# Gate/up and up products of four feed-forward layers by seven block products in place of eight

## The chip, the cores and the metric

The kernel runs on one core of a Trainium2 chip. The metric is device microseconds of one execution. Before the change, three executions took 2495.82, 2497.71 and 2503.09 us (median 2497.71).

## The reference

Two blocks of two layers work on one sequence of 512 tokens, model width 1024, float32. Each layer is a mixer (left as it is by the change) and a feed-forward part. In the first block that is (`hybrid_layer`, cut):

```
h = rms_norm(x, mlp_norm_w)
return x + jnp.square(jax.nn.relu(h @ w_up)) @ w_down      # w_up 1024x4096, w_down 4096x1024
```

and in the second (`swiglu`):

```
return (jax.nn.silu(h @ w_gate) * (h @ w_up)) @ w_down     # gate, up 1024x2816, down 2816x1024
```

where `h` is again an RMS norm of `x`, and the result is normalised once more and added to `x`.

## The kernel before

**Layout.** Activations lie feature-major: a tile has 128 features on the partitions and 512 tokens along the free dimension, so `x` is eight tiles `x[0..7]`. A weight tile `raw` is 128 by 1024: the eight 128x128 blocks (k = 0 to 7) that make one output tile of 128 features.

**Precision.** TensorE multiplies in fp32r. Every operand is split in two parts: `hi` (a copy rounded to fp32r, ScalarE) and `lo` (the rest, `raw - hi`, VectorE or GpSimd). `mm3` (lines 321 to 323) does hi·hi, hi·lo and lo·hi into one PSUM tile. So one output tile from eight k blocks is 24 matmuls of 512 columns, each with its own 128x128 weight load.

**Weights.** `weights` (lines 260 to 271) takes one of three `raw` buffers, loads it on SP's DMA queue, makes `whi` on ScalarE (line 268) and `wlo` on VectorE or GpSimd (line 269); `whi` and `wlo` have three buffers each.

**Feed-forward.** `mlp` (first block) makes 32 up tiles per layer: product, times the norm's reciprocal `rb` with a ReLU (VectorE, line 866), square (ScalarE, 867), split into an activation tile `act` (ScalarE, 275, and GpSimd, 276). `swiglu` (second block) makes 22 pairs of a gate and an up tile: each times `rb` (VectorE, 1235 and 1237), Silu (ScalarE, 1236), product of the two (VectorE, 1238), split. `groups` sets the order of the program: up tiles in groups (four of 8; 8, 8 and 6), two tiles of the next group made ahead, then eight down products over the group's activations, each added to `x` (line 874) or to `m` (1255, 1258). A scheduler then puts the instructions of each engine in a fixed order by its own estimates; each engine runs its list in that order, and waits on semaphores.

**Start of a feed-forward part.** `pre_norm` (first block) and `post_pre_norm` (second) split `x` times the norm's gain into `xg` (eight hi/lo pairs, lines 314 and 315) and work out `rb` from the sum of squares (GpSimd for the power, line 437; `rb` to SBUF on ScalarE, 461). The first three products run interleaved over k.

Of the kernel before, what the change touches and what calls it, by code (L numbers as in the profile page):

```python
# [79 lines left out]
def host_arrays(inp):  # L80
    g = {k: np.asarray(v) for k, v in inp.items()}
    out = {}

# [77 lines left out]
class Net:  # L161
# [696 lines left out]
    def mlp(self, l):  # L858
        nc, I, x = self.nc, self.I, self.x
        xg, _, rb = self.pre_norm("mlp_norm", l)  # L860

        def up(js):
            out = []
            for ps in self.fm_tiles([(self.weights(I["w1up"][l, j], 1024, nc.vector), 0) for j in js], xg):
                t, s = self.temp(), self.temp()
# [10 lines left out]
        self.groups([8] * 4, up, down)

    def groups(self, sizes, up, down, ahead=2, together=3):

        offs = np.cumsum([0] + list(sizes))  # L880
        done = {0: up(range(together)) + sum((up([j]) for j in range(together, sizes[0])), [])}
        for g in range(len(sizes)):
            if g + 1 < len(sizes):
                done[g + 1] = sum((up([offs[g + 1] + j]) for j in range(ahead)), [])
            down(g, done.pop(g))
            if g + 1 < len(sizes):
                done[g + 1] += sum((up([offs[g + 1] + j]) for j in range(ahead, sizes[g + 1])), [])

    def out_half(self, src, acts, into=None):

# [328 lines left out]
        self.normed_x = self.post_pre_norm(m, "mix_post", 1, "ffn_pre", 1)  # L1219

    def ffn(self, l):
        with self.phase(act=16, m=8):
            self.swiglu(l)

    def swiglu(self, l):
        nc, I = self.nc, self.I
        xg, rT, rb = self.normed_x

        def up(js):
            def ws(j):  # L1230
                return [(self.weights(I[n][l, j], 1024, nc.vector), 0) for n in ("gate", "up")]

            def product(pg, pu):
                t, u = self.temp(), self.temp()
                nc.vector.tensor_mul(t, pg, rb)  # L1235
                nc.scalar.activation(t, t, AF.Silu)
                nc.vector.tensor_mul(u, pu, rb)  # L1237
                nc.vector.tensor_mul(t, t, u)  # L1238
                return self.split(t, nc.gpsimd)

            if len(js) == 1:
                return [product(*(self.fm_tiles([w], xg)[0] for w in ws(js[0])))]
            (g0, u0), (g1, u1) = ws(js[0]), ws(js[1])
            p = self.fm_tiles([g0, u0, g1], xg)
            return [product(p[0], p[1]), product(p[2], self.fm_tiles([u1], xg)[0])]

        m = []

        def down(g, acts):
            for j in range(8):  # L1250
                src = I["down01"][l, g, j] if g < 2 else I["down2"][l, j]
                ps = self.fm_tile(self.weights(src, len(acts) * 128, nc.vector), acts)
                if g == 0:
                    t = self.get("m", S)
                    nc.scalar.activation(t, ps, AF.Copy)
                    m.append(t)
                else:
                    nc.vector.tensor_add(m[j], m[j], ps)

        self.groups([8, 8, 6], up, down, together=2)  # L1260
# [29 lines left out]
```

## Time and profile before

| | |
|---|---|
| median of three executions | 2497.71 us |
| the profiled execution | 2494.83 us, of which the span of its instructions is 2493.0 us |
| TensorE matmul busy | 2404.7 us, 96% |
| VectorE, ScalarE, GpSimd busy | 1360.7, 1039.4, 619.0 us (55%, 42%, 25%) |
| mean granted TensorE clock | 0.992 |
| moved by DMA | 215.30 MB, 86 GB/s |

Busy time of TensorE counts pipelined matmuls, whose rows overlap: the pace is the distance between the starts of two matmuls, not the length of a row.

### The profile page before, as it was taken

Reading aid. Unit: us, or ns where it says so; the run is one execution under the profiler, and the core shown is the slowest. Engines: PE = TensorE matmul, PEld = TensorE weight load, DVE = VectorE, ACT = ScalarE, POOL = GpSimd, SP = SyncE. Lnnn points to the kernel's source line nnn. Section 1 sums busy time; section 2 is a strip of 40 time slices with the busy share of each in tenths; the row PEclk is TensorE's granted clock in tenths of the full one; section 3 lists DMA queues with packets and bytes.
Section 4 is the critical chain, followed back from the end, with each engine's and each line's share of the span. In section 5 each row is a group of like instructions: output and inputs, shape, how many; then the busy total and the mean of one; then the engine's idle time right before and its main releaser. Section 6 shows DMA issues by size and latency. Waiting matters only on the chain.

```text
span 2493.0 us, 29049 instructions
## 1 busy us (share of the span) xinstructions
PE 2404.7 (96%) x11217; PEld 1950.8 (78%) x11217; DVE 1360.7 (55%) x2217; ACT 1039.4 (42%) x1625; POOL 619.0 (25%) x435
## 2 busy tenths in 40 slices
PE   9899999999998999999999999999999989999997
PEld 7787788888877878888887886888886766888886
DVE  6978643333488786333347867333336765433334
ACT  5656642232365675332233564223223563322222
POOL 3465320011045742110112531100001542100101
PEclk9999999999999999999999999999999999999998
DMA  4311132222232112222222211222222322322221
GB/s 160 106 64 47 64 102 93 95 100 93 77 104 91 60 47 86 100 93 93 93 97 77 84 52 60 97 98 94 93 83 70 95 75 68 102 96 98 94 87 66
DMA packets 61513, 215.30 MB, mean 86 GB/s; under 512 B 6848, under 2 KB 6976, under 8 KB 61376
## 3 DMA queue, kind: packets, MB, share of 16 engines
q1 hardware_dynamic: 59760, 207.06, 25.0%
q0 software_dynamic: 1472, 6.29, 0.7%
q8 instruction: 88, 1.44, 0.2%
q14 instruction: 49, 0.40, 0.1%
q10 hardware_dynamic: 144, 0.11, 0.0%
HBM read 211.33 MB, written 2.10 MB: 86 GB/s over the span
## 4 chain that ended last, share of the span: by engine, by line
PE 78%; DVE 14%; ACT 4%; issue 3%; POOL 1%; DMA 0%; ACTq 0%; DVEq 0%; POOLq 0%
PE mm L323 24%; PE mm L322 24%; PE mm L321 24%; DVE x L946 1%; DVE score L647 1%; PE st L307 1%; DVE m L646 1%; PE st L308 1%; PE st L542 1%; DVE m L1143 1%; ACT xg L314 1%; DVE act L287 1%; PE av L416 1%; DVE hs L1172 1%; PE av L491 1%
## 5 line engine op out<-in xcount | busy, mean ns | idle before, releaser
L268 ACT ACTIVATE whi<-raw 128x1024 fp32r<-128x1024 f32 (+3 forms) x398 | 409.8, 1032 | 1116.7 <-PE mm L322 934.6
L323 PE MATMUL mm<-xg,wlo 128*128 128x512 f32 x1792 | 711.5, 398 | 1.7 <-DVE wlo L269 1.7
L321 PE MATMUL mm<-xg,whi 128*128 128x512 f32 x1792 | 699.1, 394 | 14.3 <-ACT xg L314 12.1
L322 PE MATMUL mm<-xg,whi 128*128 128x512 f32 x1792 | 711.3, 397 | 0.2
L321 PE MATMUL mm<-act,whi 128*128 128x512 f32 x1160 | 455.8, 395 | 11.4 <-ACT act L275 8.5
L322 PE MATMUL mm<-act,whi 128*128 128x512 f32 x1160 | 459.8, 397 | 1.4 <-POOL act L276 1.4
L323 PE MATMUL mm<-act,wlo 128*128 128x512 f32 x1160 | 460.3, 397 | 0.0
L276 POOL TENSOR_TENSOR act<-t,act 128x512 fp32r<-128x512 f32 x108 | 150.4, 1395 | 1105.6 <-ACT act L275 1077.3
L269 DVE TENSOR_TENSOR wlo<-raw,whi 128x1024 fp32r<-128x1024 f32 (+2 forms) x289 | 348.4, 1207 | 135.8 <-ACT whi L268 135.3
L321 PEld LDWEIGHTS mm<-xg,whi 128*128 128x128 f32 x1792 | 339.5, 190 | 99.1 <-ACT xg L314 20.3
L322 PEld LDWEIGHTS mm<-xg,whi 128*128 128x128 f32 x1792 | 337.1, 188 | 82.9 <-DVE xg L315 6.6
L323 PEld LDWEIGHTS mm<-xg,wlo 128*128 128x128 f32 x1792 | 336.7, 188 | 76.2 <-DVE wlo L269 4.1
L269 POOL TENSOR_TENSOR wlo<-raw,whi 128x1024 fp32r<-128x1024 f32 (+3 forms) x109 | 257.3, 2362 | 296.0 <-ACT whi L268 284.7
L321 PEld LDWEIGHTS mm<-act,whi 128*128 128x128 f32 x1160 | 220.4, 190 | 64.6 <-ACT act L275 10.9
L322 PEld LDWEIGHTS mm<-act,whi 128*128 128x128 f32 x1160 | 218.3, 188 | 54.3 <-DVE act L276 2.3
L323 PEld LDWEIGHTS mm<-act,wlo 128*128 128x128 f32 x1160 | 218.1, 188 | 47.4
L874 DVE TENSOR_TENSOR x<-x,mm 128x512 f32<-128x512 f32 x64 | 44.0, 688 | 206.2 <-PE mm L323 206.2
L866 DVE SCALAR_TENSOR_TENSOR t<-mm,rb 128x512 f32<-128x512 f32 x64 | 44.1, 691 | 198.8 <-PE mm L323 198.6
L1237 DVE TENSOR_TENSOR t<-mm,rb 128x512 f32<-128x512 f32 x44 | 30.4, 691 | 141.8 <-PE mm L323 141.8
L1235 DVE TENSOR_TENSOR t<-mm,rb 128x512 f32<-128x512 f32 x44 | 30.4, 691 | 118.1 <-PE mm L323 118.1
L275 ACT ACTIVATE act<-t 128x512 fp32r<-128x512 f32 x114 | 72.1, 633 | 50.2 <-DVE t L1238 32.9
L307 PE MATMUL st<-act,act 128*128 128x128 f32 (+3 forms) x208 | 72.2, 356 | 20.8 <-DVE act L287 8.8
(226 smaller groups left out, 2641.5 us busy)
## 6 DMA issues: line engine op xcount, KB each, us to landing
raw<-in_w1up SPq DMA_DIRECT2D x64, 512.0 KB, 3.3
raw<-in_w1down SPq DMA_DIRECT2D x64, 512.0 KB, 3.2
raw<-in_gate SPq DMA_DIRECT2D x44, 512.0 KB, 3.3
raw<-in_up SPq DMA_DIRECT2D x44, 512.0 KB, 3.2
raw<-in_w1fm SPq DMA_DIRECT2D x41, 512.0 KB, 3.3
raw<-in_down SPq DMA_DIRECT2D x32, 512.0 KB, 3.2
raw<-in_odin SPq DMA_DIRECT2D x16, 512.0 KB, 3.3
raw<-in_w1out SPq DMA_DIRECT2D x16, 384.0 KB, 3.0
```

Of the source, the lines that this page charges most:

```text
L268: nc.scalar.activation(hi[:, sl], raw[:, sl], AF.Copy)
L269: (low or nc.gpsimd).tensor_sub(lo[:, sl], raw[:, sl], hi[:, sl].bitcast(F))
L275: nc.scalar.activation(hi, t, AF.Copy)
L276: (low or nc.vector).tensor_sub(lo, t, hi.bitcast(F))
L307: mm(ps, a[:, rows], b[hh][:, cols], start=True, stop=False, skip_group_check=True)
L321: mm(ps, w[0], a[0], start=first, stop=False, skip_group_check=True)
L322: mm(ps, w[0], a[1], start=False, stop=False, skip_group_check=True)
L323: self.last_mm = mm(ps, w[1], a[0], start=False, stop=last, skip_group_check=True)
L866: nc.vector.scalar_tensor_tensor(t, ps, 0.0, rb, op0=OP.max, op1=OP.mult)
L874: nc.vector.tensor_add(x[j], x[j], ps)
L1235: nc.vector.tensor_mul(t, pg, rb)
L1237: nc.vector.tensor_mul(u, pu, rb)
```

## The change

A pair of output tiles (up tiles j and j+1 in `mlp`, gate and up tile j in `swiglu`) times the 512 tokens is seen as a 2x2 block product: weights a11, a12 (first tile, k = 0 to 3 and 4 to 7), a21, a22 (second tile); tokens b11, b12 (k = 0 to 3, tokens 0 to 255 and 256 to 511), b21, b22 (k = 4 to 7). Eight block products become seven, with sums ahead and behind (`seven`; in the new listing its products are numbered here 1 to 7 in the order of the code). A block product is 12 matmuls of 256 columns.

- `token_sums`, once per layer: ScalarE copies `x` times the gain (8 of 128x512), GpSimd makes 16 sums of 128x256, then 4 splits of 128x1024 (ScalarE `tok` hi, VectorE `tok` lo).
- `pair_weights`, once per pair: the two `raw` tiles; GpSimd makes four sums of 128x512 (s1, s2 in one buffer, s3, s4 in another; two such buffers, `sum`); splits of a11|a12 (`whi`, `wlo`), s1|s2 and s3|s4 (`shi`, `slo`, three buffers in `mlp`, two in `swiglu`) and a22.
- `seven`: three PSUM tiles, seven products; a copy to `r` and one to `t` on ScalarE, five adds of 128x256 on VectorE; `post` then works from SBUF.
- Pairs run interleaved: products 1 to 3 of a pair, then 6 and 7 of the pair before, then 4 and 5.
- Per layer 13 pairs of up tiles in `mlp` (tiles 0 to 3, 30 and 31 stay plain) and 19 pairs in `swiglu` (j = 0, 1 and 21 stay plain): 64 pairs in all. They come in runs of 3, 4, 4 and 2 (`mlp`) and 5, 6, 6 and 2 (`swiglu`), between them a group's down products.
- The down products of the second block come in groups of 6, 6, 6 and 4 activations (before 8, 8 and 6), with weights of 128x768 and 128x512.
- The descriptor scratch is 4096 bytes in place of 8192; `act` has 10 and 8 buffers in place of 20 and 16.

The diff, cut:

```diff
+    def token_sums(self, x, g):
+        nc, out = self.nc, []
+        for k in range(4):
+            b = [self.temp() for _ in range(2)]
+            for i in range(2):
+                nc.scalar.activation(b[i], x[k + 4 * i], AF.Copy, scale=g(k + 4 * i))
+            (b11, b12), (b21, b22) = [(t[:, :256], t[:, 256:]) for t in b]
+            f = self.get("sum", 2 * S)
+            t1, t2, t3, t4 = [f[:, 256 * i:256 * i + 256] for i in range(4)]
+            nc.gpsimd.tensor_sub(t1, b12, b11)
+            nc.gpsimd.tensor_sub(t2, b22, t1)
+            nc.gpsimd.tensor_sub(t3, b22, b12)
+            nc.gpsimd.tensor_sub(t4, b21, t2)
+            t = self.get("tok", 4 * S, R)
+            hi, lo = t[:, :2 * S], t[:, 2 * S:]
+            nc.scalar.activation(hi, f, AF.Copy)
+            nc.vector.tensor_sub(lo, f, hi.bitcast(F))
+            out.append((hi, lo))
+        return out
...
+        a1 = parts(r0[:, :1024], 1024, ("whi", "wlo"))
+        p, q = self.get("sum", 2 * S), self.get("sum", 2 * S)
+        s1, s2, s3, s4 = p[:, :S], p[:, S:], q[:, :S], q[:, S:]
+        nc.gpsimd.tensor_add(s1, a21, a22)
+        nc.gpsimd.tensor_sub(s2, s1, a11)
+        s12 = parts(p, 1024, ("shi", "slo"))
+        nc.gpsimd.tensor_sub(s3, a11, a21)
+        nc.gpsimd.tensor_sub(s4, a12, s2)
+        s34 = parts(q, 1024, ("shi", "slo"))
+        a2 = parts(a22, 512, ("whi", "wlo"))
...
+        product(p1, a1, 0, plain(0, 0), True)
+        product(p2, s12, 1, summed(1), True)
+        product(p3, s12, 0, summed(0), True)
+        nc.scalar.activation(r1, p1, AF.Copy)
+        nc.vector.tensor_add(r2, p2, r1)
+        yield
+        t, u = self.temp(), self.temp()
+        product(p1, a1, 1, plain(1, 0), False)
+        product(p2, s34, 0, summed(2), False)
+        nc.scalar.activation(t[:, half[0]], p1, AF.Copy)
+        nc.vector.tensor_add(r3, p2, r1)
+        nc.vector.tensor_add(u[:, half[1]], p3, r3)
+        yield
+        product(p2, a2, 0, summed(3), False)
+        product(p3, s34, 1, plain(1, 1), False)
+        nc.vector.tensor_add(u[:, half[0]], p2, r1)
+        nc.vector.tensor_add(t[:, half[1]], p3, r2)
+        post(t, u)
+        yield
...
+        def both(j):
+            def post(t, u):
+                nc.vector.tensor_mul(t, t, rb)
+                nc.vector.tensor_mul(u, u, rb)
+                product(j, t, u)
+            return self.seven([I[n][l, j] for n in ("gate", "up")], xg, tok, post)
+
+        def pairs(js):
+            for j in js:
+                now = both(j)
+                next(now)
+                finish()
+                next(now)
+                left.append(now)
...
+        p = self.fm_tiles([plain("gate", 0), plain("up", 0), plain("gate", 1)], xg)
+        tok = self.token_sums(self.x, lambda c: self.v("ffn_pre", 8 * l + c))
+        product(0, tile(p[0]), tile(p[1]))
+        product(1, tile(p[2]), tile(self.fm_tiles([plain("up", 1)], xg)[0]))
+        pairs(range(2, 6))
+        for g, n in enumerate((6, 6, 6, 4)):
+            if g < 3:
+                pairs([6 * g + 6])
+            down(g, n, 0)
+            finish()
+            for j in range(1, 8):
+                down(g, n, j)
+            if g < 2:
+                pairs(range(6 * g + 7, 6 * g + 12))
```

What the scheduler's order makes of it shows at three places. Line numbers in the new order are those of the changed file: 386 and 387 are the hi and lo of a split in `pair_weights`, 393 to 397 its sums, 426 to 439 the copies and adds of `seven`, 359 to 370 `token_sums`, 1366, 1367 and 1353 the multiplications of `post`, 553 is `rb`.

VectorE, first layer of the second block, one pair in a run of gate/up tiles. Before:

```order
L1235 TENSOR_TENSOR t_13246<-mm_13196,rb_12731 128x512
L269 TENSOR_TENSOR wlo_13264<-raw_13261,whi_13263 128x1024
L1237 TENSOR_TENSOR t_13247<-mm_13221,rb_12731 128x512
L1238 TENSOR_TENSOR t_13246<-t_13246,t_13247 128x512
L269 TENSOR_TENSOR wlo_13329<-raw_13326,whi_13328 128x1024
```

Now (the pair whose s3|s4 is `slo_15756` is n, the one whose sums are `slo_15880` is n+1, and `t_15708`, `t_15709` are results of n-1):

```order
L387 TENSOR_TENSOR slo_15756<-sum_15746,shi_15755 128x1024
L438 TENSOR_TENSOR t_15709<-mm_15634,r_15636 128x256
L387 TENSOR_TENSOR wlo_15872<-raw_15867,whi_15871 128x1024
L439 TENSOR_TENSOR t_15708<-st_15635,r_15636 128x256
L1367 TENSOR_TENSOR t_15709<-t_15709,rb_14297 128x512
L1366 TENSOR_TENSOR t_15708<-t_15708,rb_14297 128x512
L387 TENSOR_TENSOR slo_15880<-sum_15875,shi_15879 128x1024
L1353 TENSOR_TENSOR t_15708<-t_15708,t_15709 128x512
L433 TENSOR_TENSOR r_15766<-mm_15764,r_15766 128x256
L387 TENSOR_TENSOR wlo_15890<-raw_15869,whi_15889 128x512
L434 TENSOR_TENSOR t_15839<-st_15765,r_15766 128x256
L427 TENSOR_TENSOR r_15896<-mm_15894,r_15896 128x256
```

Five instructions have become twelve, and the lo part of the next pair's s1|s2 stands behind the lo of this pair's s3|s4 and the results of the last.

GpSimd, the same run. Before, five pairs:

```order
L276 TENSOR_TENSOR act_13181<-t_13175,act_13181 128x512
L276 TENSOR_TENSOR act_13252<-t_13246,act_13252 128x512
L276 TENSOR_TENSOR act_13323<-t_13317,act_13323 128x512
L276 TENSOR_TENSOR act_13394<-t_13388,act_13394 128x512
L276 TENSOR_TENSOR act_13465<-t_13459,act_13465 128x512
```

Now, one pair and the first two sums of the next:

```order
L393 TENSOR_TENSOR sum_15745<-raw_15739 128x512
L394 TENSOR_TENSOR sum_15745<-sum_15745,raw_15737 128x512
L276 TENSOR_TENSOR act_15575<-t_15448,act_15575 128x512
L396 TENSOR_TENSOR sum_15746<-raw_15737,raw_15739 128x512
L397 TENSOR_TENSOR sum_15746<-raw_15737,sum_15745 128x512
L393 TENSOR_TENSOR sum_15875<-raw_15869 128x512
L394 TENSOR_TENSOR sum_15875<-sum_15875,raw_15867 128x512
```

One instruction per pair has become five; `sum_15746` takes the buffer from which the `slo` of the pair before was made.

ScalarE, start of the first `mlp`. Before:

```order
L461 ACTIVATE rb_3173<-av_3267 128x512
L867 ACTIVATE t_3290<-t_3289 128x512
L275 ACTIVATE act_3293<-t_3290 128x512
L867 ACTIVATE t_3297<-t_3296 128x512
L275 ACTIVATE act_3300<-t_3297 128x512
L867 ACTIVATE t_3304<-t_3303 128x512
L275 ACTIVATE act_3307<-t_3304 128x512
L268 ACTIVATE whi_3426<-raw_3424 128x1024
```

Now, from the second token split on (`rb_3173` stands twelve rows ahead of the first row):

```order
L369 ACTIVATE tok_3328<-sum_3323 128x1024
L359 ACTIVATE t_3331<-x_83,vec_sb 128x512
L359 ACTIVATE t_3332<-x_87,vec_sb 128x512
L359 ACTIVATE t_3343<-x_84,vec_sb 128x512
L359 ACTIVATE t_3344<-x_88,vec_sb 128x512
L369 ACTIVATE tok_3340<-sum_3335 128x1024
L369 ACTIVATE tok_3352<-sum_3347 128x1024
L958 ACTIVATE t_3386<-t_3386 128x512
L426 ACTIVATE r_3421<-mm_3418 128x256
L275 ACTIVATE act_3389<-t_3386 128x512
L386 ACTIVATE whi_3493<-raw_3489 128x1024
L386 ACTIVATE shi_3404<-sum_3400 128x1024
```

The copies of `x`, the four token splits and the first pair's `shi` come behind `rb`; in the second block the weights of the fourth plain product (`whi_14478`) come behind all four token splits in the same way.

## Rows read from the trace of the kernel before

**Rows 1.** The page, busy time by engine: us, share of the span, instructions.
```profile
PE 2404.7 (96%) x11217; PEld 1950.8 (78%) x11217; DVE 1360.7 (55%) x2217; ACT 1039.4 (42%) x1625; POOL 619.0 (25%) x435
```
**Rows 2.** The page, the chain that ended last, by engine.
```profile
PE 78%; DVE 14%; ACT 4%; issue 3%; POOL 1%; DMA 0%; ACTq 0%; DVEq 0%; POOLq 0%
```
**Rows 3.** TensorE in two stretches: 96 matmuls of 256 columns; 355 of 512 (feed-forward).
```profile
core 0: us, PE busy (x), PEclk, DMA share, GB/s
1376.70:1388.05 11.35, 11.34 (x96) 1.00 0.34 109
1558.00:1640.00 82.00, 82.00 (x355) 1.00 0.29 97
```
**Rows 4.** ScalarE groups by shape: count, then busy us, mean ns; last a timeline row.
```profile
L268 ACT ACTIVATE whi<-raw 128x1024 fp32r<-128x1024 f32 x351 | 371.1, 1059 | 1031.5 <-PE mm L322 874.4 <-issue 138.8 <-PE mm L323 6.5
L275 ACT ACTIVATE act<-t 128x512 fp32r<-128x512 f32 x114 | 72.1, 633 | 50.2 <-DVE t L1238 32.9 <-DVE t L1008 10.6 <-DVE pr L1000 3.2
L314 ACT ACTIVATE xg<-x,vec_sb 128x512 fp32r<-128x512 f32 x56 | 39.7, 717 | 56.4 <-DVE x L946 51.9 <-DVE x L856 4.5
...
1552.68 1.28 ACT L1236 ACT_TABLE_LOAD   x1 [1.91 <-DVE t L1235]
```
**Rows 5.** VectorE groups by shape; the third reads one operand from PSUM.
```profile
L269 DVE TENSOR_TENSOR wlo<-raw,whi 128x1024 fp32r<-128x1024 f32 x264 | 324.4, 1230 | 123.1 <-ACT whi L268 122.6
L1238 DVE TENSOR_TENSOR t<-t,t 128x512 f32<-128x512 f32 x44 | 30.4, 692 | 5.6 <-ACT t L1236 1.7
L547 DVE TENSOR_TENSOR pl<-st,ph 128x256 fp32r<-128x256 f32 x32 | 13.2, 413 | 1.8 <-ACT ph L546 1.8
```
**Rows 6.** GpSimd groups by shape.
```profile
L269 POOL TENSOR_TENSOR wlo<-raw,whi 128x1024 fp32r<-128x1024 f32 x87 | 215.9, 2482 | 248.3 <-ACT whi L268 237.0 <-issue 8.3 <-DVE mn L524 2.9
L276 POOL TENSOR_TENSOR act<-t,act 128x512 fp32r<-128x512 f32 x108 | 150.4, 1395 | 1105.6 <-ACT act L275 1077.3 <-issue 28.3
L276 POOL TENSOR_TENSOR pl<-t,ph 128x256 fp32r<-128x256 f32 x8 | 7.0, 876 | 11.9 <-ACT ph L275 11.7
```
**Rows 7.** Timelines, VectorE beside GpSimd at three moments: start us, us, engine.
```profile
331.23 3.81 POOL L276 TENSOR_TENSOR act<-t,act 128x512 fp32r<-128x512 f32 x3 [9.23 <-ACT act L275]
334.51 1.61 DVE L269 TENSOR_TENSOR wlo<-raw,whi 128x1024 fp32r<-128x1024 f32 x1 [0.36 <-ACT whi L268]
...
1529.59 1.29 POOL L406 TENSOR_TENSOR acc<-acc,t 128x512 f32<-128x512 f32 x1 [1.97 <-ACT t L400]
1529.62 1.80 DVE L946 TENSOR_TENSOR x<-x,m 128x512 f32<-128x512 f32 x1
...
1590.07 1.22 DVE L269 TENSOR_TENSOR wlo<-raw,whi 128x1024 fp32r<-128x1024 f32 x1
1590.90 1.54 POOL L276 TENSOR_TENSOR act<-t,act 128x512 fp32r<-128x512 f32 x1 [9.61 <-ACT act L275]
```
**Rows 8.** DMA issues: KB each, median us from issue to landing.
```profile
raw<-in_gate SPq DMA_DIRECT2D x44, 512.0 KB, 3.3
```
**Rows 9.** Timelines at the start of the first `mlp` and the first `swiglu`.
```profile
327.99 0.60 ACT L461 ACTIVATE rb<-av 128x512 f32<-128x512 f32 x1
329.14 2.08 DVE L866 SCALAR_TENSOR_TENSOR t<-mm,rb 128x512 f32<-128x512 f32 x3
333.46 0.69 DVE L866 SCALAR_TENSOR_TENSOR t<-mm,rb 128x512 f32<-128x512 f32 x1 [2.25 <-PE mm L323]
...
1546.87 1.02 POOL L437 TENSOR_TENSOR rstd<-var,mhalf 128x4 f32<-128x4 f32 x1 [6.22 <-DVE var L422]
1549.79 0.50 PE L323 MATMUL mm<-xg,wlo 128*128 128x512 f32 x1 [0.25 <-DVE wlo L269]
```
**Rows 10.** Windows: all five engines' busy time, then the clock; below, TensorE alone.
```profile
1530.00:1536.00 6.00, 4.40 (x17) 2.81 (x17) 5.74 (x6) 2.49 (x4) 2.16 (x2) 1.00 0.00 0
...
2034.00:2043.00 9.00, 0.72 (x2) 0.76 0.19 58
2043.00:2050.00 7.00, 7.00 (x26) 0.82 0.00 0
```

More of the change, by code (lines that the diff above doesn't have):

```diff
@@ L574, in hybrid @@
             self.mixers(l)
-        with self.phase(act=20):
+        with self.phase(act=10, tok=4, sum=2, shi=3, slo=3, r=2):
             self.mlp(l)
@@ L876, in mlp @@
[L876 to L887, printed above, removed]
+        acts = {}
@@ new lines, in down, with finish @@
+        def down(g, j):
+            ps = self.fm_tile(self.weights(I["w1down"][l, g, j], 1024, nc.vector), [acts[8 * g + k] for k in range(8)])
+            nc.vector.tensor_add(x[j], x[j], ps)
+        left = []
+        def pairs(js):
[5 more added lines that the diff above has]
+                left.append(now)
+        def finish():
+            while left:
+                next(left.pop())
+        up(range(3))
@@ L1221, in ffn @@
     def ffn(self, l):
-        with self.phase(act=16, m=8):
+        with self.phase(act=8, m=8, tok=4, sum=2, shi=2, slo=2, r=2):
             self.swiglu(l)
@@ L1227, in swiglu @@
         xg, rT, rb = self.normed_x
[L1229 to L1260, printed above, removed]
+        acts, m, left = {}, [], []
@@ new lines, in product, with tile, plain, both @@
+        def product(j, t, u):
+            nc.scalar.activation(t, t, AF.Silu)
+            nc.vector.tensor_mul(t, t, u)
+            acts[j] = self.split(t, nc.gpsimd)
+        def tile(ps):
+            t = self.temp()
+            nc.vector.tensor_mul(t, ps, rb)
+            return t
+        def plain(n, j):
+            return self.weights(I[n][l, j], 1024, nc.vector), 0
+        def both(j):
+            def post(t, u):
[3 more added lines that the diff above has]
+            return self.seven([I[n][l, j] for n in ("gate", "up")], xg, tok, post)
@@ new lines, in pairs, with finish, down @@
+        def pairs(js):
+            for j in js:
+                now = both(j)
+                next(now)
+                finish()
+                next(now)
+                left.append(now)
+        def finish():
+            while left:
+                next(left.pop())
+        def down(g, n, j):
+            src = I["down012"][l, g, j] if g < 3 else I["down3"][l, j]
+            ps = self.fm_tile(self.weights(src, n * 128, nc.vector), [acts[6 * g + k] for k in range(n)])
+            if g == 0:
+                t = self.get("m", S)
+                nc.scalar.activation(t, ps, AF.Copy)
+                m.append(t)
+            else:
+                nc.vector.tensor_add(m[j], m[j], ps)
@@ new lines, in swiglu @@
+        p = self.fm_tiles([plain("gate", 0), plain("up", 0), plain("gate", 1)], xg)
[4 more added lines that the diff above has]
+        for g, n in enumerate((6, 6, 6, 4)):
+            if g < 3:
+                pairs([6 * g + 6])
+            down(g, n, 0)
+            finish()
+            for j in range(1, 8):
+                down(g, n, j)
+            if g < 2:
+                pairs(range(6 * g + 7, 6 * g + 12))
+            elif g == 2:
+                pairs([19, 20])
+                t = tile(self.fm_tile(plain("gate", 21)[0], xg))
+                finish()
+                product(21, t, tile(self.fm_tile(plain("up", 21)[0], xg)))
```

71 lines of the change are left out of this document (57 added, 14 removed).

## The prediction, made before the changed kernel ran

> **What bounds the kernel now.** The page first: TensorE is busy 96% of the span, the others 25 to 55% [rows 1], and the chain that ended last runs over TensorE for 78% [rows 2]. The feed-forward stretches are solid matmul: 355 of 512 columns in 82.00 us, one each 0.231 us; 96 matmuls of 256 columns elsewhere in the kernel take 11.35 us, one each 0.119 us [rows 3]. So columns can be saved at half the price of a 512. Averages of the other engines say little: the question is which wait ends last inside a pair, for which I read the groups by shape [rows 4 to 6], the places where VectorE and GpSimd meet [rows 7], and the starts of the feed-forward parts [rows 9].
>
> **The change, part by part.**
>
> *Matmuls.* A pair cost 48 x 0.231 = 11.09 us and now has 84 x 0.119 = 10.00 us of matmul (one block product 1.43). That is 1.09 us each, 64 pairs, **-70 us** if nothing waits. The Trainium skill, "TensorE: Matmul & The Clock Gate", section "Back-to-back issue gap", gives about 131 ns for a sustained matmul of 512 columns with its weight load and 81 ns for 128. An estimate between them, 98 ns at 256, would make a pair go from 48 x 131 = 6.3 us to 84 x 98 = 8.2 us, and the change a loss of 123 us by itself. The trace differs at both widths measured here, and the measurement decides.
>
> *Work beside it, per gate/up pair.* VectorE: three lo splits of 1.23, one of 0.69, five adds of 0.41, three multiplications of 0.69 [rows 5]: 8.5 us. GpSimd: four sums and one activation, 1.29 each when undisturbed [rows 7]: 6.5 us. ScalarE some 5.7. Each is below 10 us alone; three things spoil it.
>
> *The port.* A VectorE instruction with both inputs in SBUF and a GpSimd instruction do not overlap: an add beside a GpSimd sum took 1.80 us, 0.54 after GpSimd's end; a `wlo` of 1.23 took 1.61 and ended 1.08 after GpSimd's (335.04); the other way round, a GpSimd split of 1.29 ended 1.15 after the `wlo` it met [rows 7]. VectorE reading PSUM shows no such stretching (0.41 for 256 columns, [rows 5]).
>
> *Buffers and queues.* In `swiglu` `shi` has two buffers, so s3|s4 of pair n can be split only after product 7 of pair n-1, two products before it is needed; s1|s2 of n+1 stands behind it on ScalarE and VectorE. `sum` has two buffers, so GpSimd's s3 of n+1 starts when the `slo` of n is done. I follow one cycle from T, the issue of the last matmul of product 7 of n-1 (us): result seen 0.22; hi of s3|s4 +1.06 = 1.28; lo +1.22 and a hop = 2.55. There GpSimd takes the port for s3, to 3.9. VectorE's next add reads PSUM; its `wlo` for a1 of n+1 then ends at 3.9 + 1.08 = 4.95. s4 takes the port in the shadow of the second PSUM add, to 6.1; the two multiplications of the pair before end at 6.65 and 7.3, the `slo` of s1|s2 at **8.55**. TensorE has meanwhile done product 4, waited 0.9 for the lo of product 5, some 1.1 for `wlo` in product 1, and stands at the third matmul of product 2; 46 matmuls are left to the next product 7: 46 x 0.119 = 5.47. A cycle is 14.0, taken as 14.1, against 10.0: 4.1 lost. Behind s4 GpSimd waits for the next raw tile: its buffer is free at 6.1, landing takes 3.3 [rows 8], two sums end by 12, before they are needed; the load is hidden, with 2 us to spare. The cycle repeats in a run of b pairs b-2 times: 3+4+4+0 = 11 per layer, 22 in all: **+90 us**. The last pair of each of the 8 runs still waits 1.0 for its lo: **+8**.
>
> In `mlp` `shi` has three buffers. In a run's first cycle only `wlo` of a1 is late (hi 1.28, hi of a1 2.34, `slo` 2.55, add 2.96, `wlo` 4.2 where product 1 wants it at 3.1): +1.2. In the second, the last pair's second raw tile lands at 4.2 + 3.3 = 7.5, then two activation splits and two sums go over GpSimd (4 x 1.29, to 12.7), hi of the sums 13.8, hi of a1 14.9, and `wlo` after s4 has left the port, 17.2 against 14.1: +3.3 with the hops. Runs of 3, 4, 4, 2: 10 per layer, **+20**.
>
> *Token sums.* 16 sums of 128x256 on GpSimd; none like it but [rows 6]'s third, 0.88; half of 1.29 is 0.65. I take 0.75, so 12 us per layer, and they begin late. First `mlp`, as ScalarE's order has them behind `rb` (328.6, [rows 9]): ReLU from 329.1, square, copy [rows 4]: the first sum at 331.2. Then three activation splits stand on GpSimd, to 336.4; 15 sums (11.2), 2.3 for lo splits that take the port, 2.2 for copies of `x` that stand behind a token split on ScalarE: 352.1. s1 and s2 of the first pair 2.6 and 1.1 of port: 355.8; hi 357; lo behind another `wlo` 359.3. TensorE has done its plain tiles at 333.2 (VectorE takes the last at 333.46 [rows 9]) and has 32 matmuls more that it may do, 3.8 us: it stands 22 us. The second pair's sums, behind these, cost 5 more. In `swiglu` the fourth plain product began before 1549.8 [rows 9], from 1548.8; now its weights stand on ScalarE behind all token splits: reciprocal root at 1547.9, 16 sums 12, waits for copies and port 4.5, hi 1.06, table load 1.28, Silu 0.63, hi of the weight 1.06 = 1568.5: 20 us. Two of each: **+94**. After a standstill of nine us the granted clock averaged 0.82 over the next seven [rows 10], 2.5 us at 1.2 in place of 2.4 GHz, 1.3 us lost; four times: **+5**.
>
> *At nothing.* Down products: the same 528 matmuls per layer; 8 more loads, splits and adds (0.69) lie under products of 18 x 0.231 = 4.2 us and, in the last group, 2.8 us; uncovered, the adds would cost 8 x 0.69 x 2 = 11 us. The smaller scratch serves GpSimd's few DMAs in the mixers.
>
> **Sum.** -70 + 90 + 8 + 20 + 94 + 5 = +147 on the profiled execution's 2494.8, so 2642; the median stands 2.9 above it. I forecast **2645 us**.
>
> **Rivals.**
> (1) *All of it is covered, faster.* The place is the stretch from product 7 to the `slo` of s1|s2. If it took 4.5 us (10.0 - 5.47) or less in place of 8.55, and the token sums fitted under the plain products, -70 remains: 2428. It decides at 5.6 us, where a pair costs its old 11.09. For it: no engine has 10 us of work per pair. Against it: the order puts five VectorE and two GpSimd instructions into that stretch, and their durations are rows.
> (2) *The port costs nothing*, because GpSimd's sums happen to fall under PSUM adds and idle time. The cycle is then the plain sum, 12.65 (+2.65, 58), `mlp` 16, starts 22 and 16 (76): -70 + 58 + 8 + 16 + 76 + 5 = +93: 2591. For it: in the trace of before most `wlo` rows run at 1.23 [rows 5]; against it, GpSimd had one split per pair then and has five or six now.
> (3) *The starts cost half*, if the token sums go under plain products better than the queues say: 2598.
> (4) *The clock falls inside the runs.* TensorE stands some 4 of 14 us. At 1.2 GHz the 46 matmuls of a cycle take 5.5 us more, 22 cycles, 120 us: 2765. Against it: at 4.40 busy of 6.00 the clock stayed at full speed [rows 10].
>
> **How the numbers follow.** Forecast 0.56, (2) 0.18, (3) 0.10, (4) 0.05; (1) 0.08; a cover that by chance just pays for the saving, no change, 0.03. Some 0.3% is what a measurement of this kernel can tell from none. So faster 0.08, the same 0.03, slower 0.89. The range takes in (2) and (3) and half of each start and cycle cost below, 2555; above, token sums at 0.88 (+2 per start and the port waits that come with them, 15), one more GpSimd instruction per cycle in VectorE's way (22 x 1.25 = 27) and `mlp` runs twice as late (20): 2707, set at 2710.
>
> **What would show it.** Right: products of 256 columns at 0.119; gaps on TensorE before the third matmul of product 2 of some 2.4 us, ended by line 387 of VectorE; runs of gate/up pairs with product 7 every 14 us; `slo`, `wlo` and multiplications stretched beside lines 393 to 397 of GpSimd; 20 us and more of TensorE idle at the start of each feed-forward part, ended by the pair's `shi` or the fourth product's `whi`. Wrong: a spacing above 0.132 per matmul (11.09 / 84), which would be TensorE's own loss; product 7 every 10 us; a full TensorE at the starts.

## The result, and the profile after

The changed kernel takes 2598.45 us (median of 4 runs, 2592.7 to 2604.44) against 2500.4 for the kernel before in the same comparison: a ratio of **1.0394, 95% interval 1.0363 to 1.0425**. It is slower, as forecast, by 98 us where the forecast was 147. The profiled execution has a span of 2590.8 us, 97.8 more than the one before.

Busy time by engine and the chain that ended last, from the page of the changed kernel; they answer to [rows 1] and [rows 2].

```profile
PE 2375.4 (92%) x13521; PEld 2040.4 (79%) x13521; DVE 1702.5 (66%) x2713; ACT 1216.1 (47%) x1945; POOL 1062.8 (41%) x755
...
PE 63%; DVE 21%; ACT 5%; POOL 5%; issue 5%; DMA 1%; POOLq 0%; ACTq 0%; DVEq 0%; SPq 0%
```

TensorE's share of the chain fell from 78% to 63%, VectorE's rose from 14% to 21% and GpSimd's from 1% to 5%: TensorE now waits for the work beside it. For what it waits, the view of TensorE's waits says (us in total, times, the longest); the first, second and fifth of these rows have no counterpart before, the third one of 1.1 us.

```profile
PE mm L323 <- DVE slo L387: 38.9, 26, 2.4
PE mm L321 <- ACT r L426: 34.2, 3, 17.0
PE mm L321 <- ACT whi L268: 32.6, 3, 16.0
PE mm L321 <- ACT xg L314: 12.1, 15, 0.8
...
PE mm L323 <- DVE wlo L387: 7.8, 4, 2.0
```

The first row is nearly all the runs of gate/up pairs, the second the starts of the two `mlp` layers, the third those of the two `swiglu` layers, the fifth the runs of up/up pairs; the fourth stood there before.

For a ledger I added up the starts of successive matmuls over each whole trace. A step that is over 0.35 us longer than usual for its width counts as a wait, the smaller excess as stretched. Sorted by the granted clock, 10 us of the stretched are matmuls at the lower clock before, 36 after; the rest is small excess at full clock, much the same in both.

| us | usual spacing | waits | stretched |
|---|---|---|---|
| before | 2340 | 86 | 63 |
| after | 2270 | 224 | 94 |

So the saving is there in full, -70, and 138 us of waits and some 30 of stretched matmuls, 26 of them at the lower clock, are laid on it: +98.

**A cycle of gate/up pairs.** Four engines around one cycle in the first `swiglu`, from its timelines (start us, us, engine, line): TensorE's last matmul of product 7 and the third matmul of product 2 of the pair after the next, then ScalarE, VectorE, GpSimd.

```profile
1735.44 0.28 PE L323 MATMUL st<-xg,slo 128*128 128x256 f32 x1
1742.24 0.39 PE L323 MATMUL mm<-tok,slo 128*128 128x256 f32 x1 [1.73 <-DVE slo L387]
...
1732.86 1.06 ACT L386 ACTIVATE shi<-sum 128x1024 fp32r<-128x1024 f32 x1 [1.42 <-PE st L323]
1735.70 1.06 ACT L386 ACTIVATE shi<-sum 128x1024 fp32r<-128x1024 f32 x1 [0.43 <-PE st L322]
...
1733.95 2.35 DVE L387 TENSOR_TENSOR slo<-sum,shi 128x1024 fp32r<-128x1024 f32 x1 [1.85 <-ACT shi L386]
1736.55 2.20 DVE L387 TENSOR_TENSOR wlo<-raw,whi 128x1024 fp32r<-128x1024 f32 x1
1739.01 1.43 DVE L1367 TENSOR_TENSOR t<-t,rb 128x512 f32<-128x512 f32 x1
1740.37 0.68 DVE L1366 TENSOR_TENSOR t<-t,rb 128x512 f32<-128x512 f32 x1
1740.97 1.21 DVE L387 TENSOR_TENSOR slo<-sum,shi 128x1024 fp32r<-128x1024 f32 x1
...
1736.37 1.29 POOL L396 TENSOR_TENSOR sum<-raw,raw 128x512 f32<-128x512 f32 x1 [1.16 <-DVE slo L387]
1737.64 2.26 POOL L397 TENSOR_TENSOR sum<-raw,sum 128x512 f32<-128x512 f32 x1
```

Read it from product 7 on. The `slo` of s3|s4 is finished at 1736.30, before product 5 wants it. GpSimd's s3 (line 396) takes the port, which is what the prediction calls that which VectorE and GpSimd use one at a time; `wlo`, 1.23 alone, takes 2.20 and ends 1.09 after s3. GpSimd's s4 then takes 2.26 beside `wlo` and ends 1.15 after it, and the multiplication of line 1367 takes 1.43. Only then comes the `slo` of s1|s2, to 1742.18, 6.74 after product 7, and product 2 goes on 0.06 later.

**The starts.** Timelines of the first `mlp` and, the last row, of the first `swiglu`.

```profile
331.22 0.74 POOL L363 TENSOR_TENSOR sum<-t 128x256 f32<-128x256 f32 x1 [8.46 <-ACT t L359]
331.93 3.91 POOL L276 TENSOR_TENSOR act<-t,act 128x512 fp32r<-128x512 f32 x3
335.80 0.72 POOL L364 TENSOR_TENSOR sum<-t,sum 128x256 f32<-128x256 f32 x1
...
349.92 0.72 POOL L366 TENSOR_TENSOR sum<-t,sum 128x256 f32<-128x256 f32 x1
...
352.57 0.58 PE L321 MATMUL mm<-xg,whi 128*128 128x256 f32 x1 [17.03 <-ACT r L426]
...
1608.76 0.80 PE L321 MATMUL mm<-xg,whi 128*128 128x512 f32 x1 [16.02 <-ACT whi L268]
```

The first token sum begins at 331.22, three activation splits take GpSimd to 335.84, and the sixteenth sum ends at 350.64; TensorE has stood since 335.5. What it waits for in the end is ScalarE's copy `r` (line 426), which stands behind the token splits in ScalarE's order, and these wait for the sums.

**The clock.** Windows of TensorE alone (us, busy and count, granted clock, DMA share, GB/s): the matmuls behind the wait of the first `mlp`, behind that of the first `swiglu`, and three windows around one wait of 2.38 us inside a run.

```profile
352.60:356.40 3.80, 3.60 (x15) 0.50 0.00 0
1608.80:1615.80 7.00, 5.96 (x13) 0.50 0.34 88
...
1840.00:1843.00 3.00, 2.71 (x23) 1.00 0.00 0
1843.00:1846.00 3.00, 0.90 (x4) 0.78 0.51 152
1846.00:1849.00 3.00, 3.00 (x19) 0.65 0.32 119
```

Half of full speed is 1.2 GHz. Not only the starts end in it: in seven of the 22 full cycles of gate/up pairs a wait inside the run (1.9 to 2.5 us) is followed by it too, and each of the seven loses some 1.5 us.

### The profile page after: what moved, and what is told of

Its sections match the earlier page's. It is cut to its first block, busy times and chain, and to the rows that moved or that the text cites. A ratio compares the mean times of both kernels' runs of the same rounds, so it can differ in the third digit from the quotient of the medians.

```text
span 2590.8 us, 35121 instructions
## 1 busy us (share of the span) xinstructions
PE 2375.4 (92%) x13521; PEld 2040.4 (79%) x13521; DVE 1702.5 (66%) x2713; ACT 1216.1 (47%) x1945; POOL 1062.8 (41%) x755
## 4 chain that ended last, share of the span: by engine, by line
PE 63%; DVE 21%; ACT 5%; POOL 5%; issue 5%; DMA 1%; POOLq 0%; ACTq 0%; DVEq 0%; SPq 0%
PE mm L323 18%; PE mm L322 17%; PE mm L321 17%; DVE wlo L387 2%; PE st L322 2%; PE st L321 2%; PE st L323 2%; DVE slo L387 1%; DVE t L1367 1%; DVE x L1067 1%; ACT shi L386 1%; DMA raw<-in_w1up 1%; DVE score L739 1%; DVE t L1366 1%; PE st L307 1%
## 5 line engine op out<-in xcount | busy, mean ns | idle before, releaser
L268 ACT ACTIVATE whi<-raw 128x1024 fp32r<-128x1024 f32 (+2 forms) x286 | 277.8, 973 | 536.9 <-PE mm L322 361.3
L321 PE MATMUL mm<-xg,whi 128*128 128x512 f32 (+1 forms) x1280 | 448.1, 356 | 80.3 <-ACT r L426 34.2
L323 PE MATMUL mm<-xg,wlo 128*128 128x512 f32 (+1 forms) x1280 | 453.7, 355 | 11.1 <-DVE wlo L387 7.8
L322 PE MATMUL mm<-xg,whi 128*128 128x512 f32 (+1 forms) x1280 | 454.1, 355 | 0.2 <-DVE xg L315 0.2
L321 PEld LDWEIGHTS mm<-xg,whi 128*128 128x128 f32 x1280 | 244.3, 192 | 121.3 <-ACT r L426 34.9
L387 DVE TENSOR_TENSOR slo<-sum,shi 128x1024 fp32r<-128x1024 f32 x128 | 176.2, 1377 | 229.9 <-ACT shi L386 220.4
L322 PEld LDWEIGHTS mm<-xg,whi 128*128 128x128 f32 x1280 | 245.2, 192 | 38.1 <-DVE xg L315 6.6
L386 ACT ACTIVATE shi<-sum 128x1024 fp32r<-128x1024 f32 x128 | 135.8, 1061 | 272.3 <-POOL sum L394 169.5
L322 PEld LDWEIGHTS mm<-act,whi 128*128 128x128 f32 x1160 | 218.8, 189 | 52.8 <-DVE act L276 2.3
L269 DVE TENSOR_TENSOR wlo<-raw,whi 128x1024 fp32r<-128x1024 f32 (+3 forms) x177 | 201.6, 1139 | 76.5 <-ACT whi L268 75.7
L323 PE MATMUL mm<-tok,slo 128*128 128x256 f32 x512 | 150.6, 294 | 38.9 <-DVE slo L387 38.9
L387 DVE TENSOR_TENSOR wlo<-raw,whi 128x1024 fp32r<-128x1024 f32 (+1 forms) x128 | 153.6, 1202 | 9.3 <-ACT whi L386 9.3
L321 PE MATMUL mm<-tok,shi 128*128 128x256 f32 x512 | 148.6, 290 | 9.4 <-DVE r L427 6.8
```

The costliest lines, as they stand in the source:

```text
L268: nc.scalar.activation(hi[:, sl], raw[:, sl], AF.Copy)
L269: (low or nc.gpsimd).tensor_sub(lo[:, sl], raw[:, sl], hi[:, sl].bitcast(F))
L321: mm(ps, w[0], a[0], start=first, stop=False, skip_group_check=True)
L322: mm(ps, w[0], a[1], start=False, stop=False, skip_group_check=True)
L323: self.last_mm = mm(ps, w[1], a[0], start=False, stop=last, skip_group_check=True)
L386: nc.scalar.activation(hi[:, :width], t, AF.Copy)
```

## The experiments

All ratios are to the kernel before in the same comparison; its medians in the four comparisons are 2500.40 (the change), 2497.10 (e1 to e4), 2497.42 (e5 to e8) and 2498.05 us (e9 to e11), so a difference between rows of two comparisons is good to some 3 us. "Run" is the time from product 7 of the first pair to product 7 of the last of the six pairs that lead from one down group to the next, in the middle of the first `swiglu`. Without a wait that is four times 84 x 0.119 and, for the last pair, which has matmuls of a down product in it, 48 x 0.119 + 18 x 0.231: 49.9 us. The change has 58.9 (1723.38 to 1782.32). Waits and stretched are the ledger's columns.

| | median us | ratio (95%) | run, us | waits | stretched |
|---|---|---|---|---|---|
| the change | 2598.45 | 1.0394 (1.0363 to 1.0425) | 58.9 | 224 | 94 |
| e1 no s3, s4 | 2518.62 | 1.0081 (1.0060 to 1.0102) | 50.8 | 167 | 79 |
| e2 groups alone | 2498.24 | 1.0006 (0.9991 to 1.0020) | none | 92 | 66 |
| e3 token sums on VectorE | 2570.44 | 1.0290 (1.0267 to 1.0312) | 60.7 | 193 | 101 |
| e4 `slo` first | 2598.38 | 1.0397 (1.0372 to 1.0423) | 60.1 | 228 | 96 |
| e5 s3, s4 on VectorE | 2582.46 | 1.0337 (1.0316 to 1.0358) | 58.8 | 223 | 83 |
| e6 all four on VectorE | 2524.75 | 1.0109 (1.0092 to 1.0126) | 52.9 | 173 | 76 |
| e7 token sums early too | 2484.01 | 0.9944 (0.9926 to 0.9962) | 52.9 | 129 | 80 |
| e8 one more plain pair | 2486.84 | 0.9951 (0.9935 to 0.9967) | 52.8 | 131 | 78 |
| e9 s1, s2 on VectorE | 2541.0 | 1.0170 (1.0153 to 1.0187) | 54.7 | 186 | 80 |
| e10 best, a | 2482.81 | 0.9940 (0.9924 to 0.9956) | 52.8 | 124 | 81 |
| e11 best, b | 2468.57 | 0.9882 (0.9864 to 0.9899) | 52.8 | 115 | 74 |

### e2: the down groups of six alone

```diff
-                now = both(j)
-                next(now)
-                finish()
-                next(now)
-                left.append(now)
+                t = tile(self.fm_tile(plain("gate", j)[0], xg))
+                product(j, t, tile(self.fm_tile(plain("up", j)[0], xg)))
```

(likewise in `mlp`, and no token sums.)

> The down groups of six of the second block alone: every gate, up and up/up tile is a plain product of 512 columns again, and no sums are made; order of tiles, buffer counts and the smaller scratch as in the change. Theory A: the groups cost nothing, as their extra eight loads, splits and adds per layer are covered: 2500 us, within 0.3% of the kernel before. Rival: part of the 98 us comes from here, by uncovered adds or loads or by the smaller number of activation buffers: 2511 us (eight adds of 0.69 twice) or more.

2498.24 us, no difference from before. The groups, the smaller scratch and the buffer counts cost nothing; the 98 us belong to the block products.

### e1: without GpSimd's s3 and s4

```diff
-        nc.gpsimd.tensor_sub(s3, a11, a21)
-        nc.gpsimd.tensor_sub(s4, a12, s2)
-        s34 = parts(q, 1024, ("shi", "slo"))
+        s34 = parts(r1[:, :1024], 1024, ("shi", "slo"))
```

> The changed kernel, with GpSimd's sums s3 and s4 of the weights left out of every pair: products 5 and 7 take the split of the second raw tile in their place, so TensorE, ScalarE and VectorE issue the same instructions in the same order, and GpSimd two fewer per pair. Theory A (the port): in a run of gate/up pairs the wait in product 2 ends with the slo of s1|s2, and that is late because wlo takes 2.20 us beside s3 and the multiplication 1.44 beside s4, against 1.23 and 0.69 undisturbed. Without the two sums slo ends 1.7 us earlier: cycles of some 10.4 us in place of 12.2, 22 of them, 37 us, some 10 us of lowered clock with them, and some 3 us at each of four starts: about 2540 us, wlo and multiplication at 1.23 and 0.69. Theory B (buffers and queue order): the slo stands where ScalarE's split and VectorE's order put it, whatever GpSimd does: cycles stay at 12 us, only the starts gain, 2585 us or more.

2518.62 us, 80 less than the change, more than theory A asked for; theory B is out. TensorE's order in e1 is that of the change, matmul by matmul. The groups by line show the multiplications at their undisturbed length, while `wlo` still meets GpSimd's instructions now and then (count, busy us, mean ns; its line 1364 is line 1366 of the change):

```profile
L387 DVE TENSOR_TENSOR wlo<-raw,whi 128x1024 fp32r<-128x1024 f32 x64 | 94.4, 1475 | 11.0 <-ACT whi L386 11.0
...
L1364 DVE TENSOR_TENSOR t<-t,rb 128x512 f32<-128x512 f32 x38 | 26.0, 684 | 0.3
```

In the change the same two groups have these means:

```profile
L387 DVE TENSOR_TENSOR wlo<-raw,whi 128x1024 fp32r<-128x1024 f32 x64 | 107.0, 1672 | 8.5 <-ACT whi L386 8.5
...
L1366 DVE TENSOR_TENSOR t<-t,rb 128x512 f32<-128x512 f32 x38 | 39.0, 1026 | 0.3
```

The run falls to 50.8 us, nearly the 49.9 without waits. e1 also takes two steps out of GpSimd's own queue, and the raw tiles come free sooner by them; the shorter multiplications and `wlo` are what belongs to the port alone. In the cycle shown above these were 0.97 us (`wlo`) and 0.75 us (line 1367) over their undisturbed length, together 1.7, and TensorE's wait behind them was 1.73.

### e4: the `slo` ahead of the multiplications

The post-processing of a pair is written behind the weights of the second pair after it, and its multiplications are ordered behind that pair's `slo`:

```diff
         s12 = parts(p, 1024, ("shi", "slo"))
+        self.s12_lo = self.lo_inst
...
-                nc.vector.tensor_mul(t, t, rb)
-                nc.vector.tensor_mul(u, u, rb)
+                for b in (t, u):
+                    self.after(nc.vector.tensor_mul(b, b, rb), self.s12_lo)
```

> The changed kernel with the multiplications (or ReLUs) of a pair put off on VectorE until the slo of s1|s2 of the second pair after it has been issued; the same instructions otherwise. Theory A: slo ends 1.2 us (if s4 on GpSimd still gets the port ahead of it) to 2.0 us earlier after product 7, and product 2 waits so much less: cycles of 10.2 to 11.0 us in place of 12.2, 26 to 44 us, and 5 to 10 of lowered clock: 2545 to 2570 us. Theory B: what ends the wait is the buffer of the split or GpSimd's sums, and the order on VectorE counts for little: cycles at 12, 2590 us or more. Theory C: the delayed multiplications hold up the activations or the PSUM buffers, and the wait moves to another place: 2600 us or more.

2598.38 us: no change at all, though the wait that was aimed at shrank. TensorE's waits there:

```profile
PE mm L323 <- DVE slo L387: 14.9, 28, 0.8
PE mm L323 <- DVE wlo L387: 14.1, 15, 2.1
...
PE mm L321 <- DVE r L434: 8.4, 10, 0.8
...
PE mm L322 <- POOL act L276: 5.8, 8, 0.8
```

The waits for `slo` fell from 38.9 to 14.9 us, while those for `wlo` rose from 7.8 to 14.1, for line 434 from nothing to 8.4 and for GpSimd's activation splits from 0.8 to 5.8. The number is in theory B's range; the trace shows theory A for the place and, for the sum, theory C's wait that moves. It made me ask what the places have in common. Laid over one another without their overlap, VectorE's instructions with two inputs in SBUF and GpSimd's sums and splits of the changed kernel fill 22.7 of the 24.0 us from 1736 to 1760: one resource, which is all but full. From start to start, back to back, VectorE's cost it 1.13 (1024) and 0.60 (512), GpSimd's 1.27; a pair needs 3 x 1.13 + 4 x 0.60 + 5 x 1.27 = 12.1 us of it, and a cycle of that run takes 12.1 to 12.6. Over both layers the 22 cycles run from 10.8 to 14.1, but the short ones stand at the start of a run or behind a long one (13.63, then 10.75). I call this theory D.

### e5, e6, e9: the weight sums on VectorE

```diff
-        nc.gpsimd.tensor_add(s1, a21, a22)
-        nc.gpsimd.tensor_sub(s2, s1, a11)
+        nc.vector.tensor_add(s1, a21, a22)
+        nc.vector.tensor_sub(s2, s1, a11)
...
-        nc.gpsimd.tensor_sub(s3, a11, a21)
-        nc.gpsimd.tensor_sub(s4, a12, s2)
+        nc.vector.tensor_sub(s3, a11, a21)
+        nc.vector.tensor_sub(s4, a12, s2)
```

The lower half is e5, the upper e9, both together e6.

> The changed kernel with two of the four weight sums of every pair (s3, s4) on VectorE in place of GpSimd. Theory D (the port is full): what holds one gate/up cycle at 12.1 us is the sum of all that needs the port, from start to start of back-to-back instructions: VectorE three of 1.13 and four of 0.60, GpSimd five of 1.27, together 12.1; where the instructions stand in the queues only moves the wait (the multiplications put off: 1 to 3 us of wait per cycle in other places, the same total). A sum of 512 costs the port 1.27 on GpSimd and 0.60 on VectorE, so the port's sum becomes 10.8 and VectorE's own with its five PSUM adds of 0.33 becomes 8.6: cycles of 10.8, 22 x 1.35 = 30 us and half of the 13 us of lowered clock: 2550 to 2565 us. Rival (VectorE's queue): the wait is for an instruction that stands behind others on VectorE, and two more stand there: cycles of 12.2 to 13.4, 2600 us or more.

2582.46 us, a miss: 16 less, not 33 to 48, and the run stays at 58.8 us with the port in use 20.6 of the 25 us from 1736 to 1761 (the expectation of e9 below has 19.6). So the port's sum is not the only limit. Timelines of VectorE, GpSimd and ScalarE in e5 show another:

```profile
1744.97 1.47 DVE L397 TENSOR_TENSOR sum<-raw,sum 128x512 f32<-128x512 f32 x1
...
1750.54 1.29 POOL L393 TENSOR_TENSOR sum<-raw 128x512 f32<-128x512 f32 x1 [4.66 <-DMA raw<-in_up]
1751.91 1.61 POOL L394 TENSOR_TENSOR sum<-sum,raw 128x512 f32<-128x512 f32 x1
...
1753.55 1.06 ACT L386 ACTIVATE shi<-sum 128x1024 fp32r<-128x1024 f32 x1 [4.99 <-POOL sum L394]
```

s4 gives its raw tile back at 1746.44; the next tile lands, s1 starts at 1750.54, s2 ends at 1753.52, and ScalarE has stood 4.99 for it. The raw tiles come free too late for sums in this place. e9 moves the other two and tells this chain from the port:

> The mirror image of the run with s3 and s4 on VectorE: s1 and s2 there, s3 and s4 on GpSimd. Theory D (the port's sum alone): the same sum of 10.8 us, so the same cycles of 11.9 to 12.8 and the same time as there, 2582 us. Theory F (the chain through the raw buffers): there the port was in use 19.6 of 25 us, and s1 began some 4.2 us after s4 on VectorE had given its raw tile back (load 3.6), s1 and s2 then took 2.9 on GpSimd before ScalarE could split them. On VectorE s1 and s2 take 1.2, so this chain is 1.7 shorter: cycles of 10.8 to 11.2 us, 2540 to 2560 us.

2541.0 us, run 54.7, cycles of 11.2, with TensorE's order that of the change but for 20 of 13521 matmuls: the chain was what held e5. Then all four:

> All four weight sums of every pair on VectorE. Theory D: the port's sum is 3 x 1.13 + 8 x 0.60 + 1.27 = 9.5 us and VectorE's own 9.8, both under the 10.0 of the matmuls: cycles of 10.0 to 10.4, some 44 us less in gate/up runs, 13 of lowered clock, up to 10 in the up/up runs: 2530 to 2545 us. Rival (VectorE's busy time): its durations added up, 8.5 + 4 x 0.69 = 11.3 us, are the bound, with sums of the next pair ahead of the splits of this one: cycles of 11.3 or more, 2575 us or more.

2524.75 us, 74 less than the change, a little beyond the range of theory D; the rival, VectorE's added durations, is out. The way there is only in part the one expected: the run is 52.9 us, with cycles of 10.0 to 11.2, and the gate/up runs of both layers give 38 us where 57 were expected. The rest comes from the up/up runs, whose waits (11 us) are gone, and from the `mlp` starts (4 us each), among others. And e6 is no clean test: the scheduler changed TensorE's order as well. From the fourth pair of a gate/up run on, product 6 and a good part of 7 of the pair before stand ahead of most of products 2 and 3, so the `slo` of s1|s2 is needed later. What part of the 74 us is due to this was not tested; e1 and e9 do not have it, e7, e8, e10 and e11 do. VectorE's groups in e6:

```profile
L387 DVE TENSOR_TENSOR wlo<-raw,whi 128x1024 fp32r<-128x1024 f32 x64 | 77.9, 1217 | 1.9 <-ACT whi L386 1.9
L397 DVE TENSOR_TENSOR sum<-raw,sum 128x512 f32<-128x512 f32 x64 | 61.2, 957 | 0.6
L396 DVE TENSOR_TENSOR sum<-raw,raw 128x512 f32<-128x512 f32 x64 | 53.6, 837 | 0.0
...
L394 DVE TENSOR_TENSOR sum<-sum,raw 128x512 f32<-128x512 f32 x64 | 43.7, 683 | 0.1
```

GpSimd's sums in the change took 1.35 to 1.70 in the mean; here the same sums take 0.68 to 0.96, and `wlo` is back at 1.22.

### e3, e7, e8: the token sums

e3 replaces `nc.gpsimd` by `nc.vector` in the four sums of `token_sums` and leaves the rest as in the change.

> The changed kernel with the 16 token sums of each layer on VectorE in place of GpSimd, in the same place of the program. Theory A: GpSimd's chain of 16 sums of 0.72 us with the activation splits ahead of it is what TensorE waits for at the starts. On VectorE, idle there, a sum takes some 0.4 us: in an mlp layer TensorE goes on some 10 us earlier (at 342 in place of 352.6), in a swiglu layer some 8 us earlier; 36 us over the four and a little of the lowered clock: about 2560 us. Rival: ScalarE's queue (copies, splits of the sums, ReLU, all behind the reciprocal root) sets the start: TensorE goes on less than 3 us earlier, 2588 us or more.

2570.44 us, 28 less where some 38 were expected. In the first `mlp` TensorE went on at the moment forecast, and stood again:

```profile
342.26 0.58 PE L321 MATMUL mm<-xg,whi 128*128 128x256 f32 x1 [5.90 <-ACT r L426]
351.67 0.58 PE L321 MATMUL mm<-tok,shi 128*128 128x256 f32 x1 [6.48 <-ACT shi L386]
...
345.88 3.31 POOL L393 TENSOR_TENSOR sum<-raw 128x512 f32<-128x512 f32 x1 [9.04 <-DVE tok L370]
```

The first pair's s1 on GpSimd waited for a buffer of the token sums and then took 3.31 against VectorE. With the weight sums on VectorE too, the token sums are written ahead of the plain tiles (e7; shown for `mlp`, likewise in `swiglu`), or left where they are with one more plain pair as cover (e8):

```diff
+        tok = self.token_sums(x, lambda c: self.v("mlp_norm", 8 * l + c))
         up(range(3))
-        tok = self.token_sums(x, lambda c: self.v("mlp_norm", 8 * l + c))
```

> All weight sums and token sums on VectorE, and the token sums written ahead of the three plain tiles that open a feed-forward part, where ScalarE and VectorE stand idle for 8 us before the reciprocal root. Theory A for the starts: what TensorE stood for was the late chain of sums, so most of the 28 us (mlp) and 21 us (swiglu) per start go, 5 to 8 us stay: 70 to 80 us less than with the weight sums alone moved: 2455 to 2480 us, faster than the kernel before. Rival: the copies and splits of the sums stand ahead of the root and of the fourth plain tile's weights on ScalarE, and TensorE stands as long for these: 2510 us or more.

> All weight sums and token sums on VectorE in the places of the change, and the first pair of each layer as two plain products, 60 pairs of block products left. Theory A for the starts: with the sums on VectorE TensorE stands 7 to 10 us at a start, and two more plain tiles (11.1 us) cover that; 4 x 1.09 = 4 us of saving are given up: 2460 to 2480 us. Rival as for the early sums (ScalarE's queue): 2510 us or more.

2484.01 and 2486.84 us, both faster than the kernel before, both 4 to 7 us above the range expected. Which of the two is better they do not tell: the waits in the unchanged mixers for VectorE's line 805 (4 in each profile) are 6.6 us in e7's and 10.8 in e8's. What is left in e7, the view of TensorE's waits:

```profile
PE mm L321 <- ACT whi L268: 13.4, 3, 6.7
...
PE mm L321 <- ACT whi L386: 9.2, 2, 4.6
```

At the `swiglu` starts the rival was partly right: TensorE stood 6.7 us for ScalarE's split of the fourth plain tile, which was behind the token copies, and 4.6 for the first pair's.

### e10, e11: a better version

```diff
+        w = plain("up", 1)
         tok = self.token_sums(self.x, lambda c: self.v("ffn_pre", 8 * l + c))
...
-        product(1, tile(p[2]), tile(self.fm_tiles([plain("up", 1)], xg)[0]))
-        pairs(range(2, 6))
+        product(1, tile(p[2]), tile(self.fm_tiles([w], xg)[0]))
+        t = tile(self.fm_tile(plain("gate", 2)[0], xg))
+        product(2, t, tile(self.fm_tile(plain("up", 2)[0], xg)))
+        pairs(range(3, 6))
```

with all sums on VectorE and, in `mlp`, the token sums first. e10 has the fourth tile's weights early alone, e11 the plain pair too.

> All sums on VectorE; token sums ahead of the plain tiles in mlp; in swiglu the fourth plain tile's weights are loaded and split ahead of the token sums, where TensorE stood 6.7 and 4.6 us for ScalarE's splits. Expected: half of these 11 us go, twice: 2470 to 2478 us, 0.8 to 1.1% faster than the kernel before. Rival: the token sums come later by as much and TensorE stands for the first pair in place of the fourth tile: 2484 us.

> As the last, with the first gate/up pair of each swiglu layer as two plain products (62 pairs of block products left): 11 us of cover for the token sums at the price of 1.1 us, twice. If TensorE still stands over 2 us for the first pair there: 2466 to 2476 us, faster than the last; if not: 2 us slower than the last.

e10 is at 2482.81 us, its rival's number: the waits for the fourth tile fell to 1.4 us, and four waits of 1.0 to 2.7 us follow in each `swiglu` start, up to the first pair's product 2. e11 covers most of this (one wait of 2.6 us and one of 1.4 are left at each of these starts) and takes 2468.57 us, 1.2% under the kernel before, 5% under the change. Its page, and among its waits that belong to the change the row with the largest sum:

```profile
PE 2352.4 (95%) x13449; PEld 2016.2 (82%) x13449; DVE 1809.6 (73%) x3011; ACT 1211.6 (49%) x1937; POOL 634.5 (26%) x435
...
PE mm L323 <- DVE slo L387: 9.2, 16, 0.8
```

## Why the prediction was right, and where its steps failed

The sign, the place and the mechanism hold; the sum is 49 us too high.

- **Matmuls, -70.** Right: 2340 to 2270 us at the usual spacing. The Trainium skill, "TensorE: Matmul & The Clock Gate", section "Back-to-back issue gap", gives some 131 ns for a sustained matmul of 512 columns; here it is 231, and at 256 columns 119 where the estimate from the page was 98. The loss of 123 us by that estimate did not come.
- **Gate/up cycles, +90 forecast, 54 measured** (22 cycles from product 7 to product 7, 12.45 us in the mean, over 10.0): 40 us of waits, 11 of lowered clock, the rest a spacing a little over 0.119. The step that failed is "`shi` has two buffers, so s3|s4 of pair n can be split only after product 7 of pair n-1". In the trace the split of s3|s4 starts at 1732.86, as product 3 of the same pair ends, and the one at 1735.70, behind product 7, is that of s1|s2 of the next pair: s3|s4 follows s1|s2 in one buffer, and pairs alternate. The `slo` that I put 2.55 after product 7 was done 0.86 after it. The rest of the chain is as written: s3 taking the port from `wlo`, s4 from the multiplication, the `slo` of s1|s2 behind both, product 2 stopped at its third matmul. With 6.74 in place of 8.55, 6.74 + 5.47 = 12.2, and the trace has 12.27 for this cycle. Seven of the 22 cycles do take 13.5 to 14.1, near the forecast's 14.0, but by the lowered clock, not by the chain.
- **What the chain did not say.** e4 took away its last link and gained nothing. That the port was nearly full, 12.1 us per pair, is a sum that I could have made from [rows 5] and [rows 7] and did not: I compared each engine's own total with 10 us, and the total that mattered runs over two engines. e1 and e9 show it, e5 that it is not the only limit.
- **Last pairs, +8 forecast, none measured**: in the run's last cycle TensorE does not wait (1772.42 to 1782.32). The same wrong step.
- **Up/up runs, +20 forecast, some 13 measured**: one wait of 2.0 to 2.2 us for `wlo` in the second cycle of each run of four, as placed, and some of 0.4 to 0.7; the 1.2 us forecast for first cycles did not come.
- **Starts, +94 forecast, 83 measured.** In `mlp` 17.0 and five smaller waits, 23 in all where 27 stood; in `swiglu` 16.0 and three small ones, 19 where 20 stood. The long wait in `mlp` ends with the copy `r`, not with the pair's `shi` as the signs had it; both stand behind the token splits on ScalarE. The late chain of token sums is the cause: e3, where they only move to VectorE, gives 28 us, and e6 to e7, where they move there and ahead, 41.
- **Clock, +5 forecast, 26 measured** (of the 30 that are stretched; 11 of the 26 stand in the gate/up cycles above). The term was mis-sized twice: behind the starts the clock stayed at half for 4 to 7 us, where I took the 2.5 of [rows 10]; and it fell inside the runs, which I had left to rival 4.

Of the rivals, (2), "the port costs nothing", gave 2591, nearer to the result than the forecast, by a mechanism that e1 rules out: taking two sums from the port gave back 80 us. (3), "the starts cost half", gave 2598, the measured number, and that is luck: the starts cost 83 of 94, and what is missing from the forecast is missing mostly in the runs. (1) is what a better order can aim at: with the sums on VectorE and the starts covered, 29 of the 68 us that 62 pairs save come through in e11. (4) happened in part, some 11 of its 120 us in the gate/up runs.

## What to carry to other kernels

Two engines that exclude one another are one resource: add their work up, from start to start, before you call either idle. An elementwise sum given to the slower of the two "because it is idle" can cost twice its price in that resource; here taking two of the four sums off GpSimd, onto the busier VectorE, gave back 57 us (e9) or, where they came too late for the raw tiles, 16 (e5), and all four, with another order on TensorE, 74 (e6). Where a saving needs preparation at the head of a stage, put it ahead of the stage's first late input, or keep enough plain work in front of it to cover it.

## What was not expected of the hardware

A sum of 128x512 on GpSimd costs both engines more than VectorE's own: back to back 1.27 us of the port against 0.60, and 2.26 when blocked. The Trainium skill, "Perfetto Trace Analysis", section "Optimizing Scalar/DVE Operations", warns that moving operations between GpSimd and VectorE might not help, as they share an SBUF port; the trace agrees on the sharing, and e9 adds that towards VectorE it did help, by 57 us. For 128x256 a sum takes 0.72 on GpSimd and 0.42 on VectorE (line 366, in the change and in e3).

One wait of 2.38 us inside a run (to 1845.10) was followed by 3 us at a mean granted clock of 0.65, while another of 2.29 (to 1766.94) was followed by 1.00, as was a stretch busy for 4.40 of 6.00 us before [rows 10]; what tells them apart stays open here.
